# A hybrid encoder layer on one core: the down and output projections with the activations stationary

## The chip, the cores and the metric

One core of one Trainium2 chip runs the whole program in one launch. The metric is device time in microseconds (us): the median over 3 runs, 1913.01 us (1912.27 to 1914.91). All data are f32; S = 256 tokens, D = 2048 features, hidden width 5632, 16 heads of 128, P = 128 partitions.

## The reference

One layer of a bidirectional encoder: half a feed-forward block, token mixing with two kinds of attention heads, half a feed-forward block. Cut to what the change touches:

```python
mod = silu(c) @ w_ada + b_ada          # adaLN: nine vectors of 2048, one c per batch
sh1, sc1, gt1, sh2, sc2, gt2, sh3, sc3, gt3 = split(mod, 9)

f = swiglu(modulate(rms_norm(h, g_ffn1), sh1, sc1), w1_gate, w1_up, w1_down)
h = h + 0.5 * gt1 * f                  # down projection, gate, residual
qkv = modulate(rms_norm(h, g_mix), sh2, sc2) @ w_qkv
...                                    # attention heads, rms_norm of each head group
mix = concatenate([o_na, o_dil]) @ w_o
h = h + gt2 * mix                      # output projection, gate, residual
f = swiglu(modulate(rms_norm(h, g_ffn2), sh3, sc3), w2_gate, w2_up, w2_down)
h = h + 0.5 * gt3 * f

def rms_norm(x, g):    return x * rsqrt(mean(x * x, -1) + 1e-6) * g
def modulate(n, sh, sc): return n * (1 + sc) + sh
```

## The kernel before

**Precision.** Each f32 operand is split into a high part (cast to fp32r) and a low part (the difference). A product is hi*hi + hi*lo + lo*hi: three matmuls per pair of tiles. Activations lie as pairs (hi, lo) side by side, so a tile `nx[k]`, `hd` or `ox` is 128 x 2 x 256.

**Weight stream.** All weights come from DRAM as chunks of 128x1024 (512 KB) in one fixed order. SP issues each load into one of five raw buffers (`rw`); ACT casts it (L157, `hiw`), DVE subtracts (L161, `low`), four buffers each; PE uses it. `ws.prepare` issues these three `AHEAD` = 3 chunks ahead of the chunk that PE takes. A chunk holds eight 128x128 blocks or, for qkv, two 128x512 blocks. Every weight passes once.

**Two forms of a projection.** In the feed-forward blocks and the output projection, a weight block is stationary and the activations move: per chunk eight matmuls of 512 columns (L416, or L768: the high weights with the hi and lo activations of 256 tokens) and eight of 256 (L400, or L773: the low weights with hi). The result has features in partitions, tokens in columns, like the residual `h` (16 tiles of 128x256) and the normalised input `nx`. In qkv the activations are stationary and a 512-wide weight block moves: twelve matmuls of 512 columns per chunk (L716, L719); the result has tokens in partitions.

**Background.** The nine adaLN vectors are 144 columns of 128; each takes a 1 MB load and one DVE dot product over 2048 elements (L140), issued at a set pace between the weight chunks. A gate, scale or shift is a column, one value per partition, `m[:, d : d + 1]`.

**The two boundaries.** Edge 1 lies between the second part of the first down projection (hidden features 32 to 43; the first part has features 0 to 31) and qkv, edge 2 between the output projection and the second feed-forward block. At both, the last feature tile's update is done (L488, or L752 and L753: h + gate * psum), its square added to a running sum on DVE, a matmul with ones sums over partitions (L224, L225, `pstat`), ACT takes Ln and Exp and DVE four small ops for the reciprocal root (`rstd_from`, L183 to L187), and per feature tile DVE multiplies (L241), ACT adds the shift and casts to the hi part (L242), DVE makes the lo part (L246). Meanwhile PE runs `keep_warm`, matmuls of ones with no use (L97). The first qkv units and the first chunks of the second block take their `nx` tiles as they come.

**Order.** A planner sets the order of each engine's instructions where nothing else is said. PE's order is that of the code through the attention (`MANUAL`), and PE, DVE and ACT all follow the code around the boundaries and at the start (`BORDER`, `STARTUP`). Each engine runs its list in order.

**Tail.** The last matmuls give feature tile 15; one update of 128x256 and its store end the program.

## Time and profile before

| | |
|---|---|
| median of 3 runs | 1913.01 us (1912.27 to 1914.91) |
| profiled execution, its own time | 1912.76 us |
| its span in the profile | 1911.0 us |
| busy share PE / PEld / DVE / ACT | 99% / 87% / 79% / 47% |
| DMA | 504 MB at a mean of 264 GB/s |
| edge 1: last matmul of the down projection to the first of qkv | 766.4 to 773.3 us |
| edge 2: last of the output projection to the first of the second block | 1165.8 to 1172.4 us |

All rows quoted later come from this one profiled execution. PE is TensorE's matmuls, PEld its weight loads, which run beside the matmul before; DVE, ACT, POOL and SP are the other engines, SP only issuing DMA here. A row of a group names the line of the kernel, the engine, the operation, what it writes and reads with the shapes, how many there are, then busy time and the mean of one (in ns), then the engine's idle time before them and what ended it. A matmul's mean duration overlaps its neighbours; the distance of starts is its pace.

### The profile page before, as it was taken

The numbers are of one execution on the slowest core, as the hardware profiler recorded it, in microseconds if no ns is written. First come the engines' busy times: TensorE is split into PE (matmuls) and PEld (weight loads), VectorE is DVE, ScalarE is ACT, GpSimd is POOL, SyncE is SP. The second block draws the span as 40 slices with busy tenths as digits, with TensorE's granted clock in tenths as the row PEclk, the third lists the DMA queues.
The fourth block names the chain that finished last, engine by engine and source line by source line (L and its number), as shares of the span: only waits on it lengthen the run. The fifth ranks groups of instructions, "written<-read, shape, count | busy, mean of one in ns | idle before, by whom it ended". The sixth has DMA issues, their size and how long they took to land.

```text
span 1911.0 us, 27722 instructions
## 1 busy us (share of the span) xinstructions
PE 1900.1 (99%) x10684; PEld 1667.4 (87%) x10684; DVE 1511.1 (79%) x2074; ACT 904.2 (47%) x1319; POOL 0.7 (0%) x6
## 2 busy tenths in 40 slices
PE   9999999999999999999999999999999999999999
PEld 8888888888888888888888888888888888888888
DVE  6899999999888888888788899669866554456665
ACT  2545454433335454555556555544454443344442
POOL 0000000000000000000000000000000000000000
PEclk9999999999999999999999999999999999999999
DMA  9998889899989888697776554678865655555564
GB/s 395 405 359 310 329 299 309 312 332 390 355 324 332 317 330 290 207 336 270 267 263 207 191 157 144 202 234 312 317 200 188 196 182 194 190 186 190 189 202 136
DMA packets 120084, 504.00 MB, mean 264 GB/s; under 512 B 13328, under 2 KB 15632, under 8 KB 101520
## 3 DMA queue, kind: packets, MB, share of 16 engines
q1 hardware_dynamic: 119952, 502.24, 75.2%
q8 instruction: 83, 1.36, 0.3%
q14 instruction: 49, 0.40, 0.1%
HBM read 500.09 MB, written 2.10 MB: 263 GB/s over the span
## 4 chain that ended last, share of the span: by engine, by line
PE 94%; DVE 3%; DMA 2%; issue 1%; ACT 0%; DVEq 0%; ACTq 0%
PE pb L416 27%; PE pd L416 17%; PE pb L400 14%; PE pd L400 9%; PE pqv L716 3%; PE pqk L716 3%; PE pso L768 3%; PE pqq L716 3%; PE pa L416 3%; PE pa L590 2%; PE pqv L719 2%; PE pqk L719 2%; PE pso L773 1%; PE pa L400 1%; PE pqq L719 1%; DMA ra<-in_w_ada_dram 1%
## 5 line engine op out<-in xcount | busy, mean ns | idle before, releaser
L161 DVE TENSOR_TENSOR low<-rw,hiw 128x1024 fp32r<-128x1024 f32 x644 | 778.9, 1221 | 272.7 <-ACT hiw L157 215.2
L157 ACT CAST hiw<-rw 128x1024 fp32r<-128x1024 f32 x644 | 674.9, 1052 | 658.9 <-PE pd L416 183.6
L416 PE MATMUL pb<-nx,hiw 128*128 128x512 f32 x2424 | 572.2, 390 | 0.0
L416 PEld LDWEIGHTS pb<-nx,hiw 128*128 128x128 f32 x2424 | 447.5, 188 | 88.0
L416 PE MATMUL pd<-hd,hiw 128*128 128x512 f32 x1384 | 328.6, 390 | 0.0
L400 PEld LDWEIGHTS pb<-nx,low 128*128 128x128 f32 x2432 | 307.3, 191 | 11.4 <-DVE low L161 2.4
L400 PE MATMUL pb<-nx,low 128*128 128x256 f32 x2432 | 310.8, 283 | 1.4 <-DVE low L161 1.4
L416 PEld LDWEIGHTS pd<-hd,hiw 128*128 128x128 f32 x1384 | 254.9, 188 | 50.0 <-DVE hd L173 0.3
L140 DVE CUSTOM_DVE_ANT_0 ra<-ra,cb,vec 128x2048 f32<-128x2048 f32 x109 | 255.8, 2348 | 23.9 <-DMA ra<-in_w_ada_dram 23.8
L400 PEld LDWEIGHTS pd<-hd,low 128*128 128x128 f32 x1408 | 179.1, 191 | 5.9
L400 PE MATMUL pd<-hd,low 128*128 128x256 f32 x1408 | 181.3, 283 | 0.0
L140 DVE CUSTOM_DVE_ANT_0 rx<-rx,cb,vec 128x2048 f32<-128x2048 f32 x35 | 82.2, 2348 | 5.9 <-DMA rx<-in_w_ada_dram 5.9
L488 DVE SCALAR_TENSOR_TENSOR h<-pd,m,h 128x256 f32<-128x256 f32 x126 | 58.8, 480 | 28.8 <-PE pd L400 25.0
L416 PE MATMUL pa<-nx,hiw 128*128 128x512 f32 x288 | 72.3, 393 | 0.0
L716 PE MATMUL pqv<-hiw,nx 128*128 128x512 f32 x256 | 65.3, 398 | 2.0 <-ACT nx L242 2.0
L716 PE MATMUL pqk<-hiw,nx 128*128 128x512 f32 x256 | 65.0, 396 | 0.0
L716 PE MATMUL pqq<-hiw,nx 128*128 128x512 f32 x256 | 64.6, 394 | 0.0
L768 PE MATMUL pso<-ox,hiw 128*128 128x512 f32 x240 | 60.7, 395 | 0.0
L416 PEld LDWEIGHTS pa<-nx,hiw 128*128 128x128 f32 x288 | 51.8, 189 | 9.3
L716 PEld LDWEIGHTS pqv<-hiw,nx 128*128 128x128 f32 x256 | 48.1, 190 | 12.0 <-ACT nx L242 2.2
L716 PEld LDWEIGHTS pqq<-hiw,nx 128*128 128x128 f32 x256 | 46.8, 188 | 9.1
L716 PEld LDWEIGHTS pqk<-hiw,nx 128*128 128x128 f32 x256 | 46.5, 188 | 8.9
(154 smaller groups left out, 1396.6 us busy)
## 6 DMA issues: line engine op xcount, KB each, us to landing
ra<-in_w_ada_dram SPq DMA_DIRECT2D x109, 1024.0 KB, 7.3
rw<-in_w_b_dram SPq DMA_DIRECT2D x200, 512.0 KB, 4.6
rw<-in_w_d_dram SPq DMA_DIRECT2D x128, 512.0 KB, 4.4
rw<-in_w_c_dram SPq DMA_DIRECT2D x96, 512.0 KB, 4.5
rw<-in_w_qkv_dram SPq DMA_DIRECT2D x96, 512.0 KB, 4.7
rx<-in_w_ada_dram SPq DMA_DIRECT2D x35, 1024.0 KB, 7.6
rw<-in_w_e_dram SPq DMA_DIRECT2D x48, 512.0 KB, 4.8
rw<-in_w_a_dram SPq DMA_DIRECT2D x44, 512.0 KB, 6.0
```

The source lines that it names most:

```text
L140: dot = nc.vector.tensor_tensor_reduce(out=raw, in0=raw, in1=cb, scale=1.0, scalar=vec[:, BA + i : BA + i + 1], op0=ALU.mult, op1=ALU.add, ...
L157: cast = nc.scalar.copy(hi, raw)
L161: nc.vector.tensor_tensor(lo, raw, hi.bitcast(F32), ALU.subtract)
L400: nc.tensor.matmul(out[:, :S], weights(b, 1), r[:, 0, :], start=False, stop=stop)
L416: nc.tensor.matmul(out, w, r, start=first, stop=stop)
L488: nc.vector.scalar_tensor_tensor(h[d], part_, gate(d), h[d], ALU.mult, ALU.add)
L590: nc.tensor.matmul(pa[f][:, q, :], w[:, b * P : (b + 1) * P], full[k], start=k == 0 and q == 0, stop=k == K1 - 1 and q == 1, skip_group_ch ...
L716: nc.tensor.matmul(ps[t], nx[k][:, i, t * P : (t + 1) * P], whi[:, kk * 512 : (kk + 1) * 512], start=k + i == 0, stop=False)
L719: nc.tensor.matmul(ps[t], nx[k][:, 0, t * P : (t + 1) * P], wlo[:, kk * 512 : (kk + 1) * 512], start=False, stop=k == KT - 1)
L768: nc.tensor.matmul(ps, w, o, start=kk == 0, stop=False)
L773: nc.tensor.matmul(ps[:, :S], wlo[:, kk * P : (kk + 1) * P], ox[b * 8 + kk][:, 0, :], start=False, stop=kk == 7)
```

## The change

The two down projections and the output projection take the form that qkv already has. `tok` multiplies, per chunk, two activation tiles (stationary, 128 tokens each) with two 512-wide weight blocks: per token half four matmuls with the high weights (hi and lo activations) and two with the low. D is cut into four quarters of 512 columns (Q, QW); each quarter has one PSUM bank for each token half (t = 0, 1). The weights are laid out anew for this in DRAM.

The residual `hq` lies with tokens in partitions, four tiles of 128 x 2 x 512. It comes by a second load of x ("xt", four loads of 512 KB, issued in the first up projection). Gates, scales and shifts are needed along columns: `line_of` writes a vector's 128x16 columns to DRAM, and `rows_of` reads it back as four tiles of 128x512, the same row in each partition. Seven vectors go this way (three gates, two scales, two shifts), all on SP's queue. `update` is two DVE ops of 128x512.

The boundaries become `cross`. The last quarter's last four chunks (ST) pass in token halves: first all four for tokens 0 to 127, then for 128 to 255. An `Edge` keeps the sums of squares per token (ACT's accumulating square; three quarters summed ahead by `most`, the last added in `rstd`), multiplies each quarter by the scale row ahead of time (`scaled`), and per quarter and token half does one DVE op with reciprocal root and shift row (`normed`, L281), four PE transposes (`turned`, L286, into `pt`) and the split into hi and lo of `nx` (`split`, L188 and L189). The four chunks that come next are made ready first (two of them by `ws.extra` in tiles of half a chunk's width, each half cast and subtracted by itself, L175 and L176) and pass in token halves too (`bpass`): at edge 1 the first four qkv units, at edge 2 the first four chunks of the second feed-forward block, where a half means matmuls of 256 and 128 columns. The long rows of warming matmuls and the matmuls with ones are gone; two warming matmuls stay in each `cross`. In the attention, the head group's reciprocal root is a value per token now and goes into the output projection's `update`, in both groups.

At the end, the last quarter's four chunks also pass in token halves; the second half's update is cut in two pieces of 256 columns, each with its store. The output leaves with tokens first.

```diff
+Q = 4
+QW = D // Q
+ST = 4
...
-        nx = [cp.tile([P, 2, S], F32R, tag=f"nx{k}", name=f"nx{k}") for k in range(KT)]
+        nq = [cp.tile([P, 4, 2, S], F32R, tag=f"nq{q}", name=f"nq{q}") for q in range(Q)]
+        nx = [nq[k // 4][:, k % 4] for k in range(KT)]
...
+        def line_of(j):
+            lines[j] = dram.tile([KT, P], F32, tag=f"line{j}", name=f"line{j}")
+            nc.sync.dma_start(lines[j].rearrange("k p -> p k"), mods[j])
+        def rows_of(j, tiles):
+            flat = lines[j].rearrange("k p -> (k p)")
+            for q in range(Q):
+                nc.sync.dma_start(tiles[q], flat[q * QW : (q + 1) * QW].partition_broadcast(P))
+            return tiles
...
+        def update(ps, q, t, row, r=None, cols=slice(0, QW)):
+            x, hx = ps[:, cols], hq[q][:, t, cols]
+            if r is None:
+                nc.vector.tensor_tensor(x, x, row[q][:, cols], ALU.mult)
+            else:
+                nc.vector.scalar_tensor_tensor(x, x, r[:, t : t + 1], row[q][:, cols], ALU.mult, ALU.mult)
+            nc.vector.tensor_tensor(hx, hx, x, ALU.add)
...
+        class Edge:
...
+            def square(self, q, t, dump):
+                nc.scalar.activation(dump, hq[q][:, t, :], AF.Square, accum_out=self.ss[:, t, q : q + 1])
+            def scaled(self, q, t):
+                self.n[q, t] = self.alloc("gs")
+                nc.vector.tensor_tensor(self.n[q, t], hq[q][:, t, :], self.scale[q], ALU.mult)
+            def most(self, t):
+                a, b = self.c[:, t, 0:1], self.c[:, t, 1:2]
+                nc.vector.tensor_tensor(a, self.ss[:, t, 0:1], self.ss[:, t, 1:2], ALU.add)
+                nc.vector.tensor_tensor(a, a, self.ss[:, t, 2:3], ALU.add)
+                nc.vector.tensor_scalar(a, a, 1.0 / D, EPS, ALU.mult, ALU.add)
+                nc.vector.tensor_scalar(b, a, -0.5, None, ALU.mult)
+            def rstd(self, t):
+                a, b, u, v, r, e = (self.c[:, t, i : i + 1] for i in range(6))
+                last = self.ss[:, t, Q - 1 : Q]
+                nc.scalar.activation(u, last, AF.Ln, scale=1.0 / D, bias=a)
+                nc.vector.tensor_scalar(v, last, -0.5 / D, b, ALU.mult, ALU.add)
+                nc.scalar.activation(e, u, AF.Exp, scale=-0.5)
+                nc.vector.scalar_tensor_tensor(u, e, e, v, ALU.mult, ALU.mult)
+                nc.vector.scalar_tensor_tensor(r, u, 1.5, e, ALU.add, ALU.mult)
+            def normed(self, q, t):
+                if (q, t) not in self.n:
+                    self.scaled(q, t)
+                n = self.n[q, t]
+                nc.vector.scalar_tensor_tensor(n, n, self.c[:, t, 4:5], self.shift[q], ALU.mult, ALU.add)
+            def turned(self, q, t):
+                self.bank[q, t] = bank("pt")
+                for j in range(4):
+                    nc.tensor.transpose(self.bank[q, t][:, j * P : (j + 1) * P], self.n[q, t][:, j * P : (j + 1) * P], ident)
+            def split(self, q, t):
+                b = self.bank[q, t].rearrange("p (k s) -> p k s", k=4)
+                ts = slice(t * P, (t + 1) * P)
+                split(b, nq[q][:, :, 0, ts], nq[q][:, :, 1, ts])
...
+        def tok(ps, two, w, first, last, ts=(0, 1)):
...
+            if len(ts) == 2:
+                todo = [(t, at_t(i, j, t), whi(i)) for i in range(2) for t in ts for j in range(2)]
+                todo += [(t, at_t(i, 0, t), part_of(w[1], i * QW, QW)) for i in range(2) for t in ts]
+            else:
+                t = ts[0]
+                todo = [(t, at_t(i, 0, t), whi(i)) for i in range(2)]
+                todo += [(t, at_t(i, 0, t), part_of(w[1], i * QW, QW)) for i in range(2)]
+                todo += [(t, at_t(i, 1, t), whi(i)) for i in range(2)]
...
+            for t, l, r, st, sp_ in todo:
+                nc.tensor.matmul(ps[t], l, r, start=st, stop=sp_)
...
+        def cross(ps, twos, first, upd, edge, bpass, extra, after=None):
+            A = [ws.chunk(ST - 1 - j) for j in range(ST)]
+            for j in range(ST):
+                tok(ps, twos[j], A[j], first and j == 0, j == ST - 1, (0,))
+            edge.most(0)
+            edge.most(1)
+            ws.extra(2, extra)
+            def rest(t):
+                upd(t)
+                edge.square(Q - 1, t, ps[t])
+                edge.rstd(t)
+            def second(j):
+                tok(ps, twos[j], A[j], first and j == 0, j == ST - 1, (1,))
+            rest(0)
+            edge.normed(0, 0)
+            edge.normed(1, 0)
+            second(0)
+            ws.prep1()
+            second(1)
+            second(2)
+            edge.turned(0, 0)
+            second(3)
+            edge.turned(1, 0)
+            edge.split(0, 0)
+            edge.split(1, 0)
+            rest(1)
+            if after:
+                after()
+            ws.prep1()
+            edge.normed(0, 1)
+            B = [ws.take() for j in range(4)]
+            for j in range(3):
+                bpass(j, B[j], 0)
+            edge.turned(0, 1)
+            edge.split(0, 1)
+            bpass(3, B[3], 0)
+            keep_warm(2)
+            edge.normed(1, 1)
+            bpass(0, B[0], 1)
+            edge.turned(1, 1)
+            edge.split(1, 1)
+            edge.normed(2, 0)
+            ws.prep1()
+            bpass(1, B[1], 1)
+            edge.normed(2, 1)
+            edge.turned(2, 0)
+            edge.split(2, 0)
+            ws.prep1()
+            bpass(2, B[2], 1)
+            edge.turned(2, 1)
+            edge.split(2, 1)
+            edge.normed(3, 0)
+            ws.prep1()
+            bpass(3, B[3], 1)
+            edge.turned(3, 0)
+            edge.split(3, 0)
+            edge.normed(3, 1)
+            def end():
+                edge.turned(3, 1)
+                edge.split(3, 1)
+            return end
...
+        def ffn_down(fs, hid, row, edge=None, out=None, order=None, bpass=None, extra=None):
+            n = len(fs) // 2
+            final = fs[-1] == FT - 1
+            for q in range(Q):
+                ps = [bank(f"pd{t}") for t in range(2)]
+                twos = [(hid[fs[2 * c]], hid[fs[2 * c + 1]]) for c in range(n)]
+                def upd(t, q=q, ps=ps, cut=1):
+                    for i in range(cut):
+                        cols = slice(i * QW // cut, (i + 1) * QW // cut)
+                        update(ps[t], q, t, row, cols=cols)
+                        if out is not None:
+                            nc.sync.dma_start(out[t][:, q * QW + cols.start : q * QW + cols.stop], hq[q][:, t, cols])
+                ends = final and q == Q - 1
+                if ends and order is not None:
+                    order.enter_context(tc.manual_schedule(engines=BORDER))
+                for c in range(n - ST if ends else n):
+                    tok(ps, twos[c], ws.chunk(), c == 0, c == n - 1)
+                if ends and edge is not None:
+                    return cross(ps, twos[n - ST :], False, upd, edge, bpass, extra)
+                if ends:
+                    A = [ws.chunk() for j in range(ST)]
+                    for t in range(2):
+                        for j in range(ST):
+                            tok(ps, twos[n - ST + j], A[j], False, j == ST - 1, (t,))
+                        upd(t, cut=1 + t)
+                    return
+                for t in range(2):
+                    upd(t)
+                    if edge is not None:
+                        edge.square(q, t, ps[t])
+                        edge.scaled(q, t)
...
+            def wo_unit(u, b, q, c, st_):
+                def upd(t, ps):
+                    update(ps[t], q, t, gate, rows[b])
+                def done(ps):
+                    for t in range(2):
+                        upd(t, ps)
+                        if b == 1:
+                            edge[0].square(q, t, ps[t])
+                            edge[0].scaled(q, t)
...
-            def wo_unit(u, b, d):
...
+                def go(w):
...
+                    tok(ps, (ox[b * 8 + 2 * c], ox[b * 8 + 2 * c + 1]), w, c == 0, c == 3)
+                    if c == 3:
+                        at(u + (1 if u < END - TAIL else 0), lambda: done(ps))
...
+            def bpass2(j, w, t):
...
+                ts = slice(t * P, (t + 1) * P)
+                for half in range(2):
+                    for b in range(8):
+                        k, f, i = 2 * j + b // 4, b // 2 % 2, b % 2
+                        o = ps2[f][i].rearrange("p (i s) -> p i s", i=2)[:, :, ts]
+                        r = nx[k][:, :, ts]
+                        if half:
+                            o, r = o[:, 0, :], r[:, 0, :]
+                        nc.tensor.matmul(o, part_of(w[half], b * P, P), r, start=k == 0 and not half and t == 0,
+                                         stop=False, skip_group_check=True)
...
-        "w_o": c(g["w_o"][0].reshape(2, 8, P, KT, P).transpose(0, 3, 2, 1, 4).reshape(2 * KT, P, CW)),
+        "w_o": c(g["w_o"][0].reshape(2, 4, 2, P, Q, QW).transpose(0, 4, 1, 3, 2, 5).reshape(2 * KT, P, CW)),
+        "xt": c(g["x"][0].reshape(2, P, Q, QW).transpose(2, 1, 0, 3)),
...
-        down = g[f"w{l}_down"][0].reshape(FT, P, KT, P).transpose(2, 0, 1, 3)
+        down = g[f"w{l}_down"][0].reshape(FT // 2, 2, P, Q, QW).transpose(3, 0, 2, 1, 4)
```

DVE's list at edge 1, before: the last update (h_93 is the last feature tile), its square, a weight difference (L161), the reciprocal root (rs, rsr), and the first two normalised tiles.

```order
L488 SCALAR_TENSOR_TENSOR h_93<-pd,m_80,h_93 128x256
L207 TENSOR_TENSOR sq<-h_93 128x256
L161 TENSOR_TENSOR low<-rw,hiw 128x1024
L183 TENSOR_SCALAR rs_7110<-pstat 128x256
L185 TENSOR_TENSOR rs_7109<-rsr 128x256
L186 TENSOR_TENSOR rs_7109<-rs_7109,rs_7110 128x256
L187 SCALAR_TENSOR_TENSOR rsr<-rs_7109,rsr 128x256
L241 SCALAR_TENSOR_TENSOR nt<-h_90,m_82,rsr 128x256 x2
L246 SCALAR_TENSOR_TENSOR nx_95<-nt,m_81,nx_95 128x256
```

The same place now, from the splits of the first token half on (gs: a quarter times scale; e1c: the reciprocal root; pt: transposed; L165 is the weight difference).

```order
L165 TENSOR_TENSOR low<-rw,hiw 128x1024
L189 TENSOR_TENSOR nq_95<-pt,nq_95 128x4x128
L189 TENSOR_TENSOR nq_96<-pt,nq_96 128x4x128
L238 TENSOR_TENSOR pd_6538<-pd_6538,row_3624 128x512
L241 TENSOR_TENSOR hq_1603<-hq_1603,pd_6538 128x512
L272 TENSOR_SCALAR e1c<-e1s,e1c 128x1
L274 SCALAR_TENSOR_TENSOR e1c<-e1c 128x1
L275 SCALAR_TENSOR_TENSOR e1c<-e1c 128x1
L165 TENSOR_TENSOR low<-rw,hiw 128x1024
L281 SCALAR_TENSOR_TENSOR gs<-gs,e1c,row_6157 128x512
L189 TENSOR_TENSOR nq_95<-pt,nq_95 128x4x128
L281 SCALAR_TENSOR_TENSOR gs<-gs,e1c,row_6158 128x512
```

The second half's update stands behind a weight difference and two splits, and a further weight difference stands ahead of its first normalising op.

PE's list at edge 1 now: the last chunk of the second token half (pd), between transposes (L286), and the first halves of the qkv units (pqv; hih and loh are the half-width weight tiles).

```order
L286 MATMUL pt<-ident,gs 128x128 x4
L314 MATMUL pd_6538<-hiw,hd_6039 128x512
L314 MATMUL pd_6538<-hiw,hd_6141 128x512
...
L286 MATMUL pt<-ident,gs 128x128 x4
L314 MATMUL pqv_6704<-hih,nq_95 128x512 x2
L314 MATMUL pqv_6704<-loh,nq_95 128x512 x2
L314 MATMUL pqv_6704<-hih,nq_95 128x512 x4
L314 MATMUL pqv_6704<-loh,nq_95 128x512 x2
L314 MATMUL pqv_6704<-hih,nq_95 128x512 x2
L314 MATMUL pqv_6704<-hiw,nq_96 128x512 x2
```

The first two groups of transposes, those of token half 0, stand inside the second half's matmuls; the third, of half 1, stands behind three half units of qkv.

DVE's list at edge 2 now, ahead of the first token half's end (po is the output projection's bank, ror the head group's reciprocal root; L258 is `scaled`).

```order
L240 SCALAR_TENSOR_TENSOR po_10318<-po_10318,ror,row_9552 128x512
L241 TENSOR_TENSOR hq_1601<-hq_1601,po_10318 128x512
L258 TENSOR_TENSOR gs<-hq_1601,row_10102 128x512
L240 SCALAR_TENSOR_TENSOR po_10319<-po_10319,ror,row_9552 128x512
L241 TENSOR_TENSOR hq_1601<-hq_1601,po_10319 128x512
L258 TENSOR_TENSOR gs<-hq_1601,row_10102 128x512
L165 TENSOR_TENSOR low<-rw,hiw 128x1024
...
L176 TENSOR_TENSOR loh<-rw,hih 128x512 x4
```

The third quarter's update of both halves stands ahead of one weight difference and of the four half-width ones.

484 lines of the change are left out of this document (201 added, 283 removed).

## The prediction

> **What bounds the kernel now.** I read the page first, then the PE's own waits, then the chain of waits around the two places where it leaves the PE. The page's rows (engine, busy us, share, instructions):
>
> ```profile
> span 1911.0 us, 27722 instructions
> PE 1900.1 (99%) x10684; PEld 1667.4 (87%) x10684; DVE 1511.1 (79%) x2074; ACT 904.2 (47%) x1319; POOL 0.7 (0%) x6
> ```
>
> The PE is the bound throughout; DVE, at 79%, is the one next to it. So a change pays only by shorter PE work or by fewer holes in it. The holes lie at two boundaries: first down projection to qkv (edge 1), output projection to the second FFN (edge 2). PE in order of time (start, us, line, what, wait) at edge 1, then edge 2:
>
> ```profile
> 766.42 1.05 PE L97 MATMUL warm<-ones 128*128 128x128 f32 x8
> ...
> 773.29 3.31 PE L716 MATMUL pqv<-hiw,nx 128*128 128x512 f32 x8 [2.05 <-ACT nx L242]
> 776.40 1.50 PE L719 MATMUL pqv<-low,nx 128*128 128x512 f32 x4
> 777.74 0.39 PE L716 MATMUL pqv<-hiw,nx 128*128 128x512 f32 x1
> ```
> ```profile
> 1165.83 1.05 PE L97 MATMUL warm<-ones 128*128 128x128 f32 x8
> ...
> 1172.35 2.18 PE L407 MATMUL pb<-nx,hiw 128*128 128x256 f32 x16 [0.55 <-ACT nx L242]
> ...
> 1175.32 2.00 PE L416 MATMUL pb<-nx,hiw 128*128 128x512 f32 x8
> ```
>
> Edge 1: 777.74 - 766.42 = 11.3 us for one unit that is worth 2.72 (below), so 8.6 us lost. Edge 2: 1175.32 - 1165.83 = 9.5 for a chunk worth 2.78: 6.7 lost. Together **15.3 us**, all that the new boundaries can win. Part of edge 1 is clock; one of the windows (us, busy of PE, PEld, DVE, ACT, POOL, granted clock, DMA share, GB/s):
>
> ```profile
> 773.30:777.00 3.70, 3.70 (x10) 2.92 (x11) 3.34 (x9) 1.80 (x5) 0.00 (x0) 0.58 0.19 74
> ```
>
> After a 2.05 us wait the granted clock is 0.58: that unit takes 777.74 - 773.29 = 4.45 us, 1.7 too many.
>
> **The stream.** A weight chunk (128x1024) is now 8 matmuls of 512 columns and 8 of 256; turned, it is 12 of 512, which is what a qkv unit is already. The chain of waits (start, us) in the first down projection, the second, and qkv, and the PE's rows of ten units of the output projection:
>
> ```profile
> 710.73 3.65 PE pd L416 x16
> 714.39 1.91 PE pd L400 x16
> 716.30 3.65 PE pd L416 x16
> ```
> ```profile
> 1542.70 7.28 PE pd L416 x32
> 1549.98 3.83 PE pd L400 x32
> ```
> ```profile
> 783.35 1.81 PE pqv L716 x8
> 785.17 0.91 PE pqv L719 x4
> ```
> ```profile
> 1129.83 2.00 PE L768 MATMUL pso<-ox,hiw 128*128 128x512 f32 x8
> ...
> 1157.41 1.99 PE L768 MATMUL pso<-ox,hiw 128*128 128x512 f32 x8
> ```
>
> Two chunks in 5.57 us: 2.785 each; four in 11.11: 2.778; a qkv unit 2.72; an output unit 27.58/10 = 2.758. So 88 x 0.065 + 88 x 0.058 + 32 x 0.038 = 5.7 + 5.1 + 1.2 = **12.0 us less**. It does not multiply: six long matmuls cost nearly what four long and four short did.
>
> **The boundaries.** Normalising moves to tokens in partitions, so each quarter of 512 columns and each token half passes DVE (update: two ops; then one op with the reciprocal root), PE (four transposes), ACT and DVE (split). What was one row of 256-element ops per feature tile becomes 128x512 ops. Prices (line, engine, op, shapes, count; busy, mean ns; idle before), DVE and ACT:
>
> ```profile
> L161 DVE TENSOR_TENSOR low<-rw,hiw 128x1024 fp32r<-128x1024 f32 x644 | 778.9, 1221 | 272.7 <-ACT hiw L157 215.2 <-issue 42.9 <-PE pd L400 8.5
> L458 DVE TENSOR_TENSOR gu<-gu,pb 128x512 f32<-128x512 f32 x56 | 38.4, 686 | 4.2 <-ACT gu L457 1.4
> L752 DVE SCALAR_TENSOR_TENSOR wt<-wt,m,rsr 128x256 f32<-128x256 f32 x14 | 6.8, 483 | 0.3
> L187 DVE SCALAR_TENSOR_TENSOR rqr<-rq,rqr 128x8 f32<-128x8 f32 x8 | 1.3, 166 | 0.2
> ```
> ```profile
> L157 ACT CAST hiw<-rw 128x1024 fp32r<-128x1024 f32 x644 | 674.9, 1052 | 658.9 <-PE pd L416 183.6 <-issue 169.4 <-PE pb L416 117.1
> L172 ACT CAST th<-pT 128x512 fp32r<-128x512 f32 x16 | 9.5, 591 | 5.1 <-PE pT L800 5.1
> L823 ACT ACTIVATION_READ_ACCUMULATOR sc<-sc,mx 128x1 f32 x32 | 6.0, 188 | 0.0
> L554 ACT ACTIVATE sq<-h 128x512 f32<-128x512 f32 x8 | 4.6, 622 | 3.5 <-DMA h<-in_x_dram 3.2
> L182 ACT ACTIVATE rq<-ss,epst 128x8 f32<-128x8 f32 x8 | 2.7, 342 | 0.1
> L184 ACT ACTIVATE rqr<-rq 128x8 f32<-128x8 f32 x8 | 1.8, 230 | 0.1
> ```
>
> The op with a per-row factor at 128x512 is not in the trace: at least L458's 0.69, at most twice L752's 0.48; I take 0.75, near the first, since ops twice as wide cost less than twice. Transposes, by the PE's rows in attention:
>
> ```profile
> 1098.37 0.60 PE L841 MATMUL pP<-ident,sc 128*128 128x128 f32 x4
> 1098.73 0.36 PE L169 MATMUL psc<-th 128*128 128x256 f32 x1
> 1098.93 0.28 PE L169 MATMUL psc<-tl,th 128*128 128x256 f32 x1
> ```
>
> Four take 0.36 us and the matmul behind them 0.20 instead of 0.12: 0.44 per group, eight groups per edge, **3.5 us**, and two warm matmuls 0.24.
>
> Now the waits, with PE, DVE and ACT taken strictly in the new order, about 0.04 us from one to the next, and 0.08 of overlap between independent ops of one engine.
>
> Edge 1, from T, the end of the first token half. One half of a chunk is 1.36 us of PE. First transposes: DVE still has half-chunk differences to make until T+0.8; then multiply 0.69, add 0.69, square 0.62 + 0.19, Ln 0.34, Exp 0.23, two small 0.17, and 0.75: ready at T+4.9. The second half covers three pieces, 4.08: wait 0.8. The second half ends at T+6.7, but DVE has a weight difference and two splits before its update, to T+8.6; the chain to Exp ends at T+11.5, and ahead of the next normalising op stand B3's cast on ACT (1.05, behind Exp) and its difference on DVE (1.22): ready at T+14.4. PE has had 4.5 us of work since T+6.7 and waits **3.2**. From there each step costs DVE a weight difference, a split and a normalising op, 1.14 + 0.60 + 0.75 = 2.5 and for the last quarter one more of 0.69, against 1.36 + 0.44 = 1.8 of PE: waits 0.9, 1.9 and 0.2. Sum 7.0 + 3.5 + 0.24 = 10.8 against 8.6: **+2.2**.
>
> Edge 2 is tighter: its last quarter is only the four chunks that are halved, so quarter 2's update, square and scaling of both halves (4.3 us of DVE, squares between on ACT) begin when the halved pass begins, and A3's cast and difference stand behind them: PE waits 1.6 and 0.8 before T. Then eight small ops and four half-chunk differences bring DVE to T+2.8, so the first transposes wait 2.9; then, as above, 0.2, 2.5, 0.7, 1.5 and 3.0 (both last transposes stand ahead of the next chunks). Sum 13.2. The new first pass also has 64 matmuls of 128 columns. Rows give 0.12 above (256 columns, 1.91 us for L400's 16) and half of it below; at 0.075, by the slope from 0.228 (512) to 0.12 (256), the pass costs 1.3 more than four plain chunks. Sum 13.2 + 3.5 + 0.24 + 1.3 = 18.2 against 6.7: **+11.5**. Bounds for both edges together: 3.7 + 3.7 + 1.3 - 15.3 = -6.6 if nothing were late, +13.7 as worked out, and some 4 more if DVE's unmeasured op is 0.97.
>
> **Clock.** Edges 1 and 2 then hold about four waits of 2.5 us or more; the one of 2.05 us above brought a drop worth 1.7. DVE, not PE, is late there, so part of a drop hides: I take +1.5 in all, with 0 and 7 (four times 1.7) as bounds. The Trainium skill ("TensorE: Matmul & The Clock Gate", section "What's actually happening") lets the clock fall to half after an idle window of some 3.4 us; by it no wait here would drop it and the sum were 1.5 less, but the 2.05 us wait of this trace did, so I go by the trace.
>
> **Tail and transfers.** The end of the chain is now one op, then a store:
>
> ```profile
> 1907.86 0.48 DVE h L488
> ```
> ```profile
> rw<-in_w_d_dram SPq DMA_DIRECT2D x128, 512.0 KB, 4.4
> ...
> vec<-in_vecs_dram SPq DMA_DIRECT2D x1, 112.0 KB, 2.0
> ```
>
> Turned, the last half ends with two multiplies and two adds of 128x256, about 0.42 to 0.48 each: **+1.2**. Seven vectors go out to DRAM in 4-byte pieces (2048 each) and come back as 1 MB of rows, on SP's queue among the weight loads, and x comes a second time (2 MB). Five raw buffers are 5 x 2.72 = 13.6 us, less 4.4 landing, 1.05 and 1.22: 6.9 us of delay are free. A vector's write is 2.0 us at least (vec's landing, as many partitions) and, at a few such landings, under 7: **0**. Cover gone, each late microsecond counts in full.
>
> **Sum.** The profiled run is 1912.8 (span 1911.0 and 1.8 around it), 0.2 under the median: 1912.8 - 12.0 + 2.2 + 11.5 + 1.2 + 1.5 = 1917.2, so **1917** for the median.
>
> **Rivals.** *Faster: the halves hide the normalising.* If DVE were ahead at each half (the 0.8 and 2.8 us of leftovers at T not there, the weight splits done early), the edges cost transposes and short matmuls alone: -12.0 - 6.6 + 1.2 = -17.4, 1896; half of it 1905. For it: each chain of 4.1 us has a cover of 4.08 by design. Against it: the order puts the weight splits in front. It decides from 9 us less of waits on. *Slower still: the clock falls at every long wait*, +7 instead of +1.5: 1923. *Weights late behind vectors and rows*: a write twice the free 6.9 us costs 7 at one place: 1924; against it, packets here are many but tiny. *The turned stream is no faster* (512 columns behind each new stationary tile): +12, 1929; against it, the qkv units.
>
> **Chances.** Forecast 0.47 (own range 1912 to 1921), faster rival 0.26, clock 0.17, weights 0.06, stream 0.04. A measurement of this kernel can tell 0.2%, 3.8 us, from no change: faster (under 1909.2) 0.27, nearly all from the first rival; within 0.24; slower (over 1916.8) 0.49: half the forecast and the last three. Range 1900 to 1926.
>
> **What would show it.** Units of 2.72 us in both down projections; PE waits of 2.5 us or more on DVE's normalising op before the third group of transposes in each edge, and before A3 in edge 2; granted clock under 1 there; last DVE ops 1.2 us later. Edges without such waits would make me wrong on the fast side.

## The result and the profile after

The changed kernel takes **1958.87 us** (median of 6 runs, 1954.25 to 1961.40) against 1912.97 us of the kernel before (6 runs): ratio 1.0236, 95% interval 1.0223 to 1.0250. That is 46 us slower. The forecast was 1917 with a range of 1900 to 1926: the side was right, the size was off by 42 us. The profiled execution is one of 1957.54 us.

The page of the kernel after, its first rows: PE no longer fills the span.

```profile
span 1955.8 us, 25965 instructions
PE 1904.0 (97%) x9868; PEld 1629.5 (83%) x9868; DVE 1483.8 (76%) x1940; ACT 889.0 (45%) x1293; POOL 0.7 (0%) x6
```

The span is 44.8 longer, PE is busy only 3.9 longer, with half the clock in 27 us of it (five places). So nearly all of the rest is waiting. PE's waits, by what it waited for (us in total, times, longest):

```profile
PE pT L896 <- DVE qn L854: 13.6, 3, 8.2
PE pt L286 <- DVE gs L281: 13.0, 8, 2.9
PE pd L314 <- ACT hiw L162: 5.7, 1, 5.7
PE pb L537 <- DVE low L165: 3.7, 3, 2.1
```

Only the second row, transposes that wait for the normalising op, is the wait that the prediction had worked out. The first lies in the attention, where the prediction had nothing; the third, and the longest of the fourth (2.1 at 390 us), are late weights; the other two of the fourth, 0.5 and 1.2, also stand in the run without any vector write below.

**The stream** in a quiet stretch of the second block's first down projection, and two units of the output projection:

```profile
1594.47 1.98 PE L314 MATMUL pd<-hiw,hd 128*128 128x512 f32 x8
1596.28 1.07 PE L314 MATMUL pd<-low,hd 128*128 128x512 f32 x4
1597.19 1.98 PE L314 MATMUL pd<-hiw,hd 128*128 128x512 f32 x8
```
```profile
1090.49 2.03 PE L314 MATMUL po<-hiw,ox 128*128 128x512 f32 x8
1092.35 1.09 PE L314 MATMUL po<-low,ox 128*128 128x512 f32 x4
1093.29 2.03 PE L314 MATMUL po<-hiw,ox 128*128 128x512 f32 x8
```

A down chunk takes 1597.19 - 1594.47 = 2.72, as forecast. An output unit takes 2.80, not 2.72: 233 ns per matmul where the same form takes 227 elsewhere. That is more than the 2.758 before.

**Late weights.** ACT and PE at the start of the second part of the first down projection (in brackets: idle before, and what ended it), and SP's queue ahead of it:

```profile
699.52 1.05 ACT L162 CAST hiw<-rw 128x1024 fp32r<-128x1024 f32 x1 [1.57 <-DMA rw<-in_w_e_dram]
714.54 1.04 ACT L162 CAST hiw<-rw 128x1024 fp32r<-128x1024 f32 x1 [13.97 <-DMA rw<-in_w_e_dram]
```
```profile
708.88 1.07 PE L314 MATMUL pd<-low,hd 128*128 128x512 f32 x4
715.64 3.78 PE L314 MATMUL pd<-hiw,hd 128*128 128x512 f32 x8 [5.69 <-ACT hiw L162]
719.22 1.89 PE L314 MATMUL pd<-low,hd 128*128 128x512 f32 x4
```
```profile
688.55 6.92 SPq L117 DMA_DIRECT2D line<-m x2
695.58 5.29 SPq L156 DMA_DIRECT2D rw<-in_w_e_dram x2
```

ACT had no weights for 14 us; PE ran dry for 5.7 and then, at half clock, took 719.22 - 715.64 = 3.58 us for eight matmuls that take 1.81 in the quiet stretch above. In the queue stand the writes of two vectors, scale and shift. How long such a write takes, and how many packets under 512 bytes there are (13328 before):

```profile
DMA packets 138124, 513.38 MB, mean 262 GB/s; under 512 B 28176, under 2 KB 28688, under 8 KB 119568
...
line<-m SPq DMA_DIRECT2D x7, 8.0 KB, 15.6
```

An 8 KB write lands after 15.6 us in the median. By the landings in the trace, the two weight loads issued at 695.6 and 699.8 us landed 18.9 and 16.2 us later; ordinary ones took 4.6. SP is held as well: issuing the two writes took it 6.92 us from start to end, where the last one, at 1585 us, took 0.38, and the reads of the rows wait for the writes, with weight loads behind them in SP's list:

```profile
SPq L123 <- DMA line<-m: 15.5, 2, 9.9
```

How much of the delay comes by SP and how much by the late landings is not told apart here; the run with the write in ACT's queue shows late landings where SP issues no write.

**The attention.** DVE and PE at the end of qkv (L145 is the dot product of an adaLN column):

```profile
1096.77 2.35 DVE L145 CUSTOM_DVE_ANT_0 ra<-ra,cb,vec 128x2048 f32<-128x2048 f32 x1 [1.25 <-DMA ra<-in_w_ada_dram]
...
1100.33 2.35 DVE L145 CUSTOM_DVE_ANT_0 ra<-ra,cb,vec 128x2048 f32<-128x2048 f32 x1
...
1106.12 2.35 DVE L145 CUSTOM_DVE_ANT_0 ra<-ra,cb,vec 128x2048 f32<-128x2048 f32 x1 [1.43 <-DMA ra<-in_w_ada_dram]
```
```profile
1101.69 0.38 PE L896 MATMUL pT<-ident,kn 128*128 128x128 f32 x2
1110.24 0.47 PE L896 MATMUL pT<-ident,qn 128*128 128x128 f32 x1 [8.17 <-DVE qn L854]
```

Six columns are left over and drained in one go here (`bg_until(0)`, which both kernels have at this unit); DVE waits for their loads in its list, and the heads' q behind them. In the kernel before, the old `ffn_down` had its own `bg_until(0)` in the middle of the second part of the first down projection. The change took that call away: 22 columns were left then for the time from 800 us to edge 2, 30 now. So the last dot of the attention stood at 1057 us, and q came without a wait:

```profile
1056.56 2.35 DVE L140 CUSTOM_DVE_ANT_0 ra<-ra,cb,vec 128x2048 f32<-128x2048 f32 x1
```
```profile
1088.23 0.38 PE L800 MATMUL pT<-ident,qn 128*128 128x128 f32 x2
```

The stages, from the first matmul of each to that of the next (us, from the traces; the last four are kernels of the next section; the wait for q at the end of qkv lies behind the first output matmuls, so in the stage "output"):

| stage | before | after | no vector write | later turned write | columns moved | edge 2's cover |
|---|---|---|---|---|---|---|
| first block, up | 223.7 | 227.9 | 224.3 | 224.3 | 224.3 | 224.3 |
| down, first part | 178.1 | 177.9 | 177.3 | 180.0 | 178.0 | 178.0 |
| up, rest | 133.6 | 135.0 | 135.0 | 135.1 | 135.4 | 135.4 |
| down, rest; edge 1; first 8 qkv units | 97.5 | 107.5 | 97.7 | 99.2 | 102.8 | 95.9 |
| rest of qkv, heads | 270.7 | 275.9 | 277.3 | 276.0 | 274.2 | 274.2 |
| output, edge 2, second block's up | 462.0 | 489.2 | 488.6 | 489.4 | 478.2 | 471.7 |
| down, first part | 177.8 | 175.3 | 175.3 | 175.5 | 175.4 | 175.5 |
| up, rest | 133.4 | 133.4 | 133.4 | 133.4 | 133.4 | 133.4 |
| down, rest, to the end | 70.3 | 70.2 | 70.2 | 70.2 | 70.2 | 70.2 |

### The profile page after: what moved, and what is told of

Read it like the earlier page. It is cut to its first block, busy times and chain, and to the rows that moved or that the text cites. A ratio compares the mean times of both kernels' runs of the same rounds, so it can differ in the third digit from the quotient of the medians.

```text
span 1955.8 us, 25965 instructions
## 1 busy us (share of the span) xinstructions
PE 1904.0 (97%) x9868; PEld 1629.5 (83%) x9868; DVE 1483.8 (76%) x1940; ACT 889.0 (45%) x1293; POOL 0.7 (0%) x6
## 4 chain that ended last, share of the span: by engine, by line
PE 66%; DVE 3%; DMA 2%; ACT 1%; issue 1%; SPq 0%; ACTq 0%
PE pb L543 20%; PE pd L314 17%; PE pb L537 10%; PE pqk L314 4%; PE pqv L314 4%; PE pqq L314 4%; PE po L314 3%; DMA rw<-in_w_e_dram 1%; DMA rw<-in_w_o_dram 1%; DVE low L165 1%; PE po L185 1%; PE pt L286 0%; ACT hiw L162 0%; SPq L135 0%; PE psc L185 0%
## 5 line engine op out<-in xcount | busy, mean ns | idle before, releaser
L165 DVE TENSOR_TENSOR low<-rw,hiw 128x1024 fp32r<-128x1024 f32 x640 | 774.3, 1221 | 334.1 <-ACT hiw L162 310.8
L543 PE MATMUL pb<-nq,hiw 128*128 128x512 f32 x2032 | 495.4, 390 | 1.1 <-DVE gu L588 0.7
L543 PEld LDWEIGHTS pb<-nq,hiw 128*128 128x128 f32 x2032 | 374.3, 188 | 74.3 <-DVE gu L588 1.0
L314 PE MATMUL pd<-hiw,hd 128*128 128x512 f32 x1408 | 352.7, 391 | 6.6 <-ACT hiw L162 5.7
L314 PEld LDWEIGHTS pd<-hiw,hd 128*128 128x128 f32 x1408 | 265.9, 189 | 62.8 <-ACT hiw L162 6.1
L537 PEld LDWEIGHTS pb<-nq,low 128*128 128x128 f32 x2032 | 262.1, 192 | 13.8 <-DVE low L165 5.3
L537 PE MATMUL pb<-nq,low 128*128 128x256 f32 x2032 | 269.9, 283 | 3.7 <-DVE low L165 3.7
L145 DVE CUSTOM_DVE_ANT_0 ra<-ra,cb,vec 128x2048 f32<-128x2048 f32 x111 | 260.2, 2344 | 7.5 <-DMA ra<-in_w_ada_dram 7.5
L314 PE MATMUL pd<-low,hd 128*128 128x512 f32 x704 | 190.7, 391 | 2.0 <-DVE low L165 2.0
L314 PEld LDWEIGHTS pd<-low,hd 128*128 128x128 f32 x704 | 132.5, 189 | 30.8 <-DVE low L165 3.2
L543 PE MATMUL pb<-nq3b,hiw 128*128 128x512 f32 x336 | 90.0, 390 | 0.0
L145 DVE CUSTOM_DVE_ANT_0 rx<-rx,cb,vec 128x2048 f32<-128x2048 f32 x33 | 77.4, 2345 | 3.0 <-DMA rx<-in_w_ada_dram 2.9
L543 PE MATMUL pa<-nq,hiw 128*128 128x512 f32 x288 | 72.3, 393 | 0.0
```

The costliest lines, as they stand in the source:

```text
L145: dot = nc.vector.tensor_tensor_reduce(out=raw, in0=raw, in1=cb, scale=1.0, scalar=vec[:, BA + i : BA + i + 1], op0=ALU.mult, op1=ALU.add, ...
L165: nc.vector.tensor_tensor(lo, raw, hi.bitcast(F32), ALU.subtract)
L314: nc.tensor.matmul(ps[t], l, r, start=st, stop=sp_)
L537: nc.tensor.matmul(out[:, :S], weights(b, 1), r[:, 0, :], start=False, stop=stop, skip_group_check=self.shared)
L543: nc.tensor.matmul(out, weights(b, 0), r, start=first, stop=last and b in early, skip_group_check=self.shared)
```

## The experiments

Three theories. **W**: the write of a vector in 2048 pieces of four bytes holds the weight loads behind it. **C**: adaLN columns left over make DVE late in the attention. **D**: at the boundaries, the order of DVE's and PE's lists sets the waits, and not DVE's speed. Rivals stand with each run. All times are medians of 4 runs; the kernel before took 1913 to 1914 us beside them. Where a wait is given without a row, it is the distance of two starts on PE less the usual pace, some 0.1 to 0.2 more than the idle time in a row.

### No vector write

```diff
-            lines[j] = dram.tile([KT, P], F32, tag=f"line{j}", name=f"line{j}")
-            nc.sync.dma_start(lines[j].rearrange("k p -> p k"), mods[j])
+            return
...
-            flat = lines[j].rearrange("k p -> (k p)")
+            flat = a["w_ada"][j * KT][0, :]
```

> Leaves out the seven writes of a vector to DRAM; the rows are read, in the same shape and at the same places of the code, from the first row of one weight column block each, so gates, scales and shifts are other numbers. Theory W (a write of 2048 four-byte pieces holds the weight loads behind it): the waits of 2.25 us at 387 us and 5.86 us at 710 us and the half clock behind them go, about 11 us with them: 1944 to 1949. Rival R (the broadcast reads and the second load of x are what makes weights late): less than 3 us gained, 1956 or more. Under both, the wait of 8.4 us at 1102 us stays, if it is DVE's dots of adaLN columns that were left over (theory C); if it too is late weights, 1935.

Measured: **1946.06** (1.0169, 1.0154 to 1.0184), 12.8 us less than the changed kernel, within W's 1944 to 1949. The stage table shows where: 3.6 in the first up projection and 9.8 in the stage of edge 1. The reads of the rows and the second load of x stayed, so they are not the cause of this part. The wait at the end of qkv stayed as well (8.1 us), so that one isn't late weights.

### The write turned

```diff
-            nc.sync.dma_start(lines[j].rearrange("k p -> p k"), mods[j])
+            ps = (pair("lt")[:, 0, :] if pools["kind"] == "pair" else bank("lt"))[:KT, :P]
+            nc.tensor.transpose(ps, mods[j], ident)
+            flat = sp.tile([P, S], F32, tag="nt", name="ltc")[:KT, :P]
+            nc.scalar.copy(flat, ps)
+            nc.sync.dma_start(lines[j], flat)
```

> The computation as a whole, with one thing changed: PE transposes the 128x16 vector first, ACT copies it, and it is written as 16 pieces of 512 bytes. W: the write lands in some 2 us, the loads behind it are not held, 1945 to 1951 (seven small transposes and copies, under 2 us, against the kernel without writes). If any write with a read that waits for it on the same queue costs the same whatever its pieces: 1957 to 1960.

Measured: **1961.48**, no gain, though the write now lands in 1.4 us. PE's waits in this kernel say why:

```profile
PE lt L119 <- DVE m L150: 6.9, 1, 6.9
PE pd L319 <- ACT ltc L121: 5.4, 1, 5.4
```

`lt` is the transposed vector. Two of the seven vectors (the first and the third block's gates) are complete only just before they are needed, and the transposes stand in PE's list ahead of the down projections: PE waits there, and for a bank that ACT copies out. So the run says nothing against W; the remedy had a price of its own.

### The write in ACT's queue

```diff
-            nc.sync.dma_start(lines[j].rearrange("k p -> p k"), mods[j])
+            nc.scalar.dma_start(lines[j].rearrange("k p -> p k"), mods[j])
```

> The same writes of four-byte pieces, issued by ACT into its own queue instead of SP's. If only the order in SP's queue is what holds the weights (loads behind the write in one queue): the weight loads land in 4 to 6 us during the writes, 1945 to 1951. If the small pieces stop the DMA engines themselves for all queues: the loads are as late as before, 1956 to 1962.

Measured: **1954.70** (1953.75 to 1961.88), between the two cases and hardly better than the changed kernel. Its writes:

```profile
line<-m ACTq DMA_DIRECT2D x7, 8.0 KB, 19.8
```

The write of the first gate goes out beside the loads of SP's queue, and by the landings three weight loads issued from 341 to 344 us, in the other queue, took 14.7 to 15.2 us where the two before them took 4.4. So it isn't the order in one queue: while a write of small pieces runs, loads of another queue are late too. The next three writes go out at 449, 545 and 671 us here, far apart, and not at 689, 690 and 728; PE has no wait of over 0.8 us in the 40 us behind each, and the stage of edge 1 is 97.7 us, as with no write. So a single write was absorbed there, where two in a row emptied PE in the changed kernel; the first of all, in the up projection, cost time in both. The Trainium skill ("DMA: Bandwidth & Descriptors", section "Rules for kernel authors") says that spreading transfers over issuing engines brings no bandwidth, since all use the same 16 DMA engines. The late landings in the other queue fit shared engines; no run here measures the bandwidth.

### Columns early, with the turned write

```diff
         def begin():
-            ws.pace(0.0)
+            ws.pace(RB)
...
                 ends = final and q == Q - 1
+                if edge is not None and q == 2:
+                    bg_until(0)
+                    ws.pace(0.0)
```

> The turned write, and the adaLN columns paced through the first half of the second part of the first down projection and all drained there, as in the kernel before, so that about six fewer are left for the end of qkv. Theory C: the wait of 8.4 us at the end of qkv shrinks to 2 or less, 8 to 11 us less than the turned write alone (1936 to 1942). If that wait is late weights of the output projection: within 3 us of the turned write alone.

Measured: **1957.96**, only 3.5 us less than the turned write alone, where 8 to 11 were expected. PE's idle time between the end of qkv and edge 2 did fall, from two waits of 7.8 and 2.5 us to none, as C says. The gain was lost elsewhere: 2.0 us behind the drained dots in the down projection, 3.2 more behind edge 2, where PE waits for the PSUM banks of the second block's first chunks, and 1.2 more for the first vector's transpose; half clock covers 37.5 us in place of 34.1.

### The write turned and later

```diff
                 for c in range(n - ST if ends else n):
+                    if line is not None and (q, c) == (0, 4):
+                        line_of(line)
+                        rows_of(line, row)
...
-            rows_of(j, row)
...
-        line_of(2)
...
-        line_of(8)
```

> The turned write, with the two vectors that PE waited for (gates 1 and 3, waits of 5.6 and 7.1 us and half clock behind both) transposed and written four chunks into the down projection, where their last dot is done. W (pieces of four bytes, not writing as such, held the weights): these waits go and nothing takes their place, 1944 to 1949, as without any write. If a write and the reads behind it cost by themselves: 1953 or more.

Measured: **1947.93** (1.0184, 1.0168 to 1.0200), in the range of W. The two waits went, but not quite without a successor: the first write, at 403 us, took 7.6 us among row and weight loads, PE waited 2.0 for weights at 420 us, and a window of half clock followed (the 180.0 in the table). The writes in this kernel, the median of seven:

```profile
line<-ltc SPq DMA_DIRECT2D x7, 8.0 KB, 3.1
```

Whole computation, same vectors, pieces of 512 bytes: 11 us less than the changed kernel and 2 more than with no write at all.

### Small pieces, later

Against the kernel of the run before:

```diff
-            nc.tensor.transpose(ps, mods[j], ident)
...
-            nc.sync.dma_start(lines[j], flat)
+            nc.sync.dma_start(lines[j].rearrange("k p -> p k"), mods[j])
```

> The places of the later write, but with the pieces of four bytes of the changed kernel again. If the pieces are what costs (the write holds every load behind it for 10 to 17 us): 4 to 12 us more than the later turned write (1948), 1952 to 1960. If it was the places alone: 1946 to 1950.

Measured: **1964.57** (1.0270, 1.0251 to 1.0288), 16.6 us more than with pieces of 512 bytes, where 4 to 12 were expected. The writes take 16.8 us again, and PE's wait of 5.6 us is back. But the places are not the same: without the transposes that tie them to PE's list, the planner issues the first four writes at 355, 689, 690 and 729 us, as in the changed kernel, and not at 403, 706, 707 and 1056. So moving the lines of code doesn't move these writes, and the time alone can't tell pieces from places. The last write can: it stands in a quiet stretch of the second block's down projection in both kernels. In pieces of 512 bytes (at 1580 us) it landed after 3.1 us, and the weight load behind it after 4.9; in pieces of four (at 1592 us) after 11.8, and the load behind it after 13.0. So the pieces cost.

### Columns moved

Here "the run before" is the later turned write (1947.93), not the small pieces:

```diff
+RCX = 0.09
...
-            ws.pace(up_rate)
+            ws.pace(up_rate + RCX if begin else up_rate)
...
-COLUMNS = (..., 70, 74, 79, 85)
+COLUMNS = (..., 70, 79, 85, 91)
```

> The kernel of the run before, with about eight adaLN columns taken earlier: a pace of 0.42 in place of 0.33 columns per chunk in the second up projection of the first block, and the list of qkv units that take a column as it was in the kernel before (91 in, 74 out). Theory C: the waits of 8.0, 2.9 and 3.1 us and the half clock behind them (some 2) go: 1929 to 1934. If DVE is late in the attention for another reason: less than 5 us gained.

Measured: **1938.85** (1.0135, 1.0119 to 1.0152), 9.1 us less than the later turned write; 14 to 19 were expected. The place in question is cured: PE's wait for q at the end of qkv is

```profile
1094.70 0.33 PE L903 MATMUL pT<-ident,qn 128*128 128x128 f32 x1 [0.63 <-DVE qn L861]
```

instead of 8.2, and the stage with it 11.2 us shorter. The wait of 3.1 at 1016 us went too; column 74 is no longer taken there. But the stage of edge 1 grew by 3.6, with a new wait of 2.0 ahead of the first transposes and 1.7 at half clock. C holds; the expectation left out what edge 1 took.

### The weight splits behind

```diff
-            ws.prep1()
             edge.normed(0, 1)
+            ws.prep1()
...
             edge.turned(1, 1)
-            edge.split(1, 1)
             edge.normed(2, 0)
-            ws.prep1()
+            edge.split(1, 1)
             bpass(1, B[1], 1)
             edge.normed(2, 1)
             edge.turned(2, 0)
-            edge.split(2, 0)
             ws.prep1()
+            edge.split(2, 0)
...
```

> The kernel of the run before, with the order in both boundaries changed: the weight splits that stand ahead of the normalising ops of token half 1 and of the last two quarters go behind them. If DVE's order is what makes PE wait there (edge 1: 2.9, 0.9, 1.8 us; edge 2: 1.4, 0.5, 1.2, 3.0): 4 to 8 us less than the run before. If the chain itself is as long as PE's cover, or the splits are late then instead: within 2 us of it.

Measured: **1928.45** (1.0078, 1.0062 to 1.0094), 10.4 us less, more than the 4 to 8 expected. The waits ahead of the third and later groups of transposes went from 2.95, 0.93 and 1.82 to 1.35 alone at edge 1, and at edge 2 one of 2.3 was left of the four behind the first. No work was taken away, so it is the order of the lists, as D says.

### Edge 2's cover

```diff
-            edge.turned(0, 0)
             second(3)
+            edge.turned(0, 0)
             edge.turned(1, 0)
...
             ws.shared = True
+            ws.group, ws.turn = 1, False
```

> The kernel with the splits behind, with two more places of PE's order moved: both groups of transposes of token half 0 behind the last half chunk, and at edge 2 the last group of transposes behind one chunk of the second block, as at edge 1, in place of directly behind the group before. If PE's cover, not DVE's speed, is what is left there: the wait of 2.3 us at edge 2 goes and those of 2.0 and 2.4 us shrink by about 1 each, 3 to 5 us less than 1928. If DVE's chain ends no earlier than before and PE waits a place further on: within 2 us of 1928.

Measured: **1923.57** (1.0056, 1.0038 to 1.0074), 4.9 us less, as expected. At edge 2 the wait of 2.3 ahead of the last group went and that of 2.4 became two of 1.0 and 1.3, but the wait for PSUM banks behind the edge grew by 1.0; one window of half clock fewer than in the run before is worth up to 1.7 of the gain. At edge 1 the first two groups of transposes now wait 0.49 us together, and the third 1.01:

```profile
768.37 1.32 PE L292 MATMUL pt<-ident,gs 128*128 128x128 f32 x8 [0.49 <-DVE gs L287]
775.24 0.66 PE L292 MATMUL pt<-ident,gs 128*128 128x128 f32 x4 [1.01 <-DVE gs L287]
```

### DVE's work off the chain

```diff
-            ws.extra(2, extra)
...
             edge.normed(1, 0)
+            ws.extra(2, extra)
...
-                            edge[0].scaled(q, t)
+                            if q < 2:
+                                edge[0].scaled(q, t)
```

The four banks are also copied out ahead of the Tanh ops.

> The kernel with edge 2's cover, and three pieces of DVE and ACT work taken off the chain at the boundaries: the half-width weight splits (2.5 us of DVE) go behind the first two normalising ops, edge 2's scaling of the third quarter (1.4 us) goes to where it is first needed, and the four PSUM banks of the second block's first chunks are copied out before the Tanh table is loaded (1.28 us). If DVE's backlog at the end of token half 0 is what is left: the waits of 1.0 and 1.3 us at edge 2, 0.7 at edge 1 and 1.9 behind edge 2 shrink by 3 to 5 together, 1918 to 1921. If PE then waits for the moved splits: within 1.5 us of 1923.6.

Measured: **1926.32** (1.0073, 1.0056 to 1.0090), 2.8 us more, though the intervals of the two ratios overlap. PE's transposes at edge 2 come without a wait now, and the matmuls behind them wait instead, for the low part of nx, which stands behind the moved splits:

```profile
1173.76 1.03 PE L292 MATMUL pt<-ident,gs 128*128 128x128 f32 x8
1177.27 2.08 PE L1054 MATMUL pg<-nq,hih 128*128 128x256 f32 x8 [2.48 <-DVE nq L195]
```

PE's idle time at and behind edge 2 is the same in sum, 5.0 us against 5.2, so the rival was right: a piece that is moved back is late next. What its trace has more of in that stage is half clock: two windows behind the wait of 2.48, where the run before had one in all. The wait for the PSUM banks (1.9) stayed though the copies now come ahead of the Tanh table, so the table is not its cause; in both kernels a weight difference of 1.2 us stands on DVE ahead of the add that frees the bank.

### The update later

Each quarter's update of a down projection is held in the code until two chunks into the next quarter.

> The kernel of the run before, with each quarter's update (2.6 us of DVE in one piece) held until two chunks into the next quarter. If these blocks of DVE work, in front of the next weight differences, make the waits of 1.4 and 1.3 us in the first block's down projections and up projection: up to 3 us less than the run before. If the adaLN dots alone do: the same within 1 us.

Measured: **1927.00** (1.0068, 1.0053 to 1.0083), no difference that can be told, and the two waits of 1.4 and 1.3 us are the same. The trace shows the same order on DVE there (four ops of the update, a dot, the weight differences), so the planner undid the move and the run leaves the question open. The equal time is a sum of two changes: a third wait, for weights at 423 us, is 3.1 us idle here against 1.4, with a window of half clock behind it, and the first down part 3.6 longer; the wait of 2.48 at edge 2, the same in both, is followed by no half clock here, and that stage is 3.2 shorter.

## Why the prediction was wrong

- **Stream, -12.0:** right in the pace of the down projections, not in what they won. Units of 2.72 us, 176 of them, against 2.78, are worth between -10 and -10.8. But by the stage table the first parts won 0.2 and 2.5 us, where 64 units each should give 4.2 and 3.7: in the first, three waits for DVE's weight differences (2.0 us idle in all) and a window of half clock took the gain, in the second a wait of 0.9 most of what is missing. The prediction has no such waits. The output projection, 32 units, forecast -1.2, gave +1.3 (2.80 against 2.758). No run explains the 233 ns.
- **Edge 1, +2.2:** right. The waits were 2.95, 0.93 and 1.82, sum 5.7, against the 7.0 worked out; the 0.8 ahead of the first group did not come. With the writes gone, the stage is 0.2 longer than before; 24 chunks at 0.06 less make the boundary itself +1.7.
- **Edge 2, +11.5:** right in size. The transposes waited 2.4, 1.6, 0.5, 1.3 and 3.1, and the weights in the halved pass were late by 1.1 and 0.7, as had been worked out (1.6 and 0.8): 10.7 in these seven, of the 13.2 forecast, and 0.9 more behind the edge. The sign named beforehand, a wait of 2.5 or more ahead of the third group, came at edge 1 (2.95) but not here (1.6). The unmeasured DVE op with a per-row factor, taken as 0.75, takes this:

```profile
L281 DVE SCALAR_TENSOR_TENSOR gs<-gs,e2c,row 128x512 f32<-128x512 f32 x8 | 5.9, 746 | 0.1
```

- **Clock, +1.5:** too small in this kernel, where half clock follows the long waits that were not foreseen (half of PE's busy time in it is some 9.5 us); the boundaries' own share is two windows of 3.4 us, worth 1.7 each.
- **Tail, +1.2:** right. The end of the chain after, four ops and 1.8 us where one took 0.48:

```profile
1951.07 0.45 DVE pd L238
...
1951.54 0.43 DVE hq L241
...
1951.99 0.44 DVE pd L238
...
1952.46 0.42 DVE hq L241
```

- **Transfers, 0: the step that failed first.** The prediction priced a vector's write between 2.0 us, the landing of the 112 KB vector load, and "a few such landings, under 7", against 6.9 us of free delay. The nearest rows were loads of large pieces; none was a write of 2048 pieces. It took 15.6 in the median, the loads behind it landed 15.6 to 18.9 us after their issue in place of 4.6, and two writes stood in a row. The rival that had this mechanism ("weights late behind vectors and rows") was priced at 7 us for one place and given a chance of 0.06, because the pieces are many but tiny; the tininess is what costs. Measured where the sum had 0: 12.8 us, by the run with no write.
- **Not in the sum at all: the columns.** The diff takes `bg_until(0)` out of `ffn_down` and puts 74 for 91 in the list of units. The prediction does not mention them, so it had the waits of PE on DVE in the attention at nothing. The run with the columns moved is 9.1 us faster, and its stage after qkv 11.2. In the changed kernel PE waited for q for 8.2, 2.9 and 2.5 us. A part of the attention's delay remains after that (274.2 us against 270.7, waits of 1.5 and 1.9 for a score's op on DVE beside one of 1.3 that the kernel before has too); that it comes from DVE's ops that split the first eight heads earlier is argued from the diff, not shown.
- **The main rival** ("the halves hide the normalising") was told by the run with the splits behind and the one after it: reordering alone won 15.3 us. So the reason that the prediction gave against it, that the order puts the weight splits in front, was right, and the halves could do more than this order let them.

Of the 42 us between forecast and result, the writes are 12.8 and the columns 9.1, each by its run. The kernel with both mended, at 1938.85, is still 22 above the forecast. By the stage table against the terms of the sum, that is some 5.5 in the two first down parts (above), 5 at edge 1 (its new wait, and half clock), 6 in the output stage (slower units, and two windows of half clock), 3.5 in the attention and 2.4 in the first block's up projections. So that the change is slower was forecast for a reason that holds, the waits at the edges; most of the 46 us has others. (By the prediction's own shares the chance of slower adds up to 0.51, not 0.49.)

The best version stays some 11 us over the kernel before. By the table most of it lies in one stage: output projection, edge 2 and what follows are 9.7 us longer; the attention is 3.5 longer, the first block's up projections 2.4, and the down projections with edge 1 win 4.1. No version beat the kernel before.

## What to carry to other kernels

Price a DMA by its pieces and by what is queued with it, not by its bytes: beside 8 KB in four-byte pieces, loads of 512 KB landed 12 to 19 us after their issue in place of 4.6. A transpose and a copy ahead of the write brought its own landing from 15.6 us to a median of 1.4 to 3.1, but paid only where the transpose stands behind the work that makes its input. When a rewrite drops a function, look for what that function did besides its arithmetic: here a call that emptied a background queue; taking that work earlier again was worth 9 us in one kernel and 3.5 in another. At a boundary, first move work in the lists behind what the bound engine waits for; when no such piece is left, moving only passes the wait on.

## What the runs showed of the hardware

**The clock's windows.** In all 13 traces each stretch of half clock lasts 3.413 us or a multiple of it (but for the one at the program's end, which the record cuts off), and within a trace their starts lie whole multiples of 3.413 apart (in the kernel after: 0, 95, 116, 210 and 246 windows). The same wait of 2.79 us ahead of the third group of transposes at edge 1, in the kernel after and in the one with no vector write (window in us, then us of PE, PEld, DVE, ACT, POOL, granted clock, DMA share, GB/s); of each the window with the wait, then the next:

```profile
782.38:785.80 3.42, 1.13 (x6) 0.59 (x4) 2.03 (x5) 1.89 (x5) 0.00 (x0) 1.00 0.00 0
785.80:789.20 3.40, 2.90 (x9) 2.51 (x10) 1.57 (x3) 0.59 (x1) 0.00 (x0) 0.50 0.42 154
```
```profile
770.45:773.87 3.42, 1.59 (x8) 0.97 (x6) 1.73 (x5) 2.16 (x5) 0.00 (x0) 1.00 0.00 0
...
773.87:777.30 3.43, 2.46 (x15) 2.19 (x16) 2.06 (x4) 0.59 (x1) 0.00 (x0) 1.00 0.50 153
```

PE was busy in 0.33 of the first window, and the clock fell; in 0.46 of the second, where the wait lay across a border, and it did not. Over all traces, with the windows laid out from the first half clock of each, every window at full clock that lies inside the program and has PE busy in less than 0.44 was followed by half clock, between 0.44 and 0.57 both happened, and above 0.57 it never did. So what a wait of 2 to 3 us costs depends on where it falls. The last two runs above show it best: the same wait of 2.48 us at edge 2 was followed by two windows of half clock in one trace and by none in the other, and the stage is 472.7 us long in the first and 469.5 in the second. The Trainium skill ("TensorE: Matmul & The Clock Gate", section "What's actually happening") gives a free-running window of 3413 ns, which the traces agree with; it lets the clock fall after at least one idle window. That they do not bear out, if idle means without work: a window in which PE was busy for 0.4 of the time was enough.

**Small writes.** A write of 2048 four-byte pieces took 11.4 to 23.5 us to land, and loads of both queues were late beside it. The packets' records don't hold the time. The last write of the kernel after, issued at 1585.13, landed after 11.36 us. These are the DMA packets from 1584.5 to 1588 us, and from 1588 to 1597:

```profile
DMA packets 2152, 0.30 MB, mean 87 GB/s; under 512 B 2080, under 2 KB 2080, under 8 KB 2152
```
```profile
DMA packets 78, 0.32 MB, mean 35 GB/s; under 512 B 0, under 2 KB 0, under 8 KB 78
```

All the pieces are recorded within the first 3 us; for the 9 us that follow, one weight load is in flight beside the write (SP's next instruction reads the rows and waits for the write), and the DMA engines move 35 GB/s, against a mean of 262 over the program. That load, issued at 1586.26, landed after 12.48 us. What the engines waited for is open.
